# Weight parts, normed input and MLP activations: buffers of one kind at one byte modulo 512

## The chip, the cores and the metric

One core of one Trainium2 chip runs the whole program. The metric is the device time of one execution in microseconds; the median of three runs of the kernel before is 2125.77 us (2125.0 to 2126.07).

## The reference

Two residual layers over 256 tokens of 2048 channels, all in float32. Cut to what matters:

```python
def reference(x, positions, ...):
    for i in range(2):
        if i == 0:      # sparse attention: 16 heads, 4 kv heads, an indexer picks 64 keys a query
            x = x + _dsa_mixer(_rmsnorm(x, attn_norm_g[0]), attn_w_in[0], ..., attn_w_out[0], positions)
        else:           # (B * conv3(C * u)) @ w_out, with B, C, u = h @ w_in
            x = x + _short_conv_mixer(_rmsnorm(x, conv_norm_g[0]), conv_w_in[0], conv_w[0], conv_w_out[0])
        h = _rmsnorm(x, mlp_norm_g[i])
        a = jax.nn.relu(h @ mlp_w1[i])          # 2048 -> 8192
        x = x + (a * a) @ mlp_w2[i]             # 8192 -> 2048
    return x
```

Nearly all of the arithmetic is the products of 256 tokens with the weights.

## The kernel before

**Products.** Weights arrive in float32 by SyncE's DMAs into four `raw` tiles, two pieces in each. `split` turns a piece into two float32r parts: ScalarE writes the high part `wh` (L202), VectorE the rest `wl` (L203). The activations are held as high and low parts too: 16 `xp` tiles for the normed input (one for each 128 rows of the contraction, high parts of 256 tokens, then low parts), four `hq` tiles for four such k-tiles each (attention output, MLP hidden values, convolution output). A product is high times high, plus low times high, plus high times low. `matmuls(p)` issues piece p in one of two forms:

- tall: the weight is the stationary operand (128 columns of it), xp is streamed: L224 with `wh` on 512 columns, L225 with `wl` on 256. A piece is 4 column groups by 2 k-tiles, 8 pairs, 16 matmuls. Used for the first MLP weight and the convolution's input.
- wide: the activations are stationary, the weight is streamed: L229 (high x, `wh`), L230 (low x, `wh`), L231 (high x, `wl`), mostly 512 columns each, four triples, 12 matmuls a piece. Used on hq for the second MLP weight and both output projections, on xp for the attention input.

Each matmul comes with a weight load (LDWEIGHTS, its row in the profile is PEld), which runs beside the matmul before it.

**Order.** Everything is written out by hand, in one sequence of units: attention input (pieces 0 to 63: 16 for the indexer with column groups of 384, 384 and 336, 16 for k and v, 32 for q), attention output (64 to 95), MLP 0 (96 to 351, groups of two tall units of 8 pieces and two wide ones of 8), convolution input (352 to 447, tall), convolution output (448 to 479, wide), MLP 1 (480 to 735). After each piece, `step_all` advances the side work (norms, attention, activations) and pieces up to four ahead are split. So `wh` and `wl` have five buffers each (`AHEAD + 1`), and piece p uses buffer 0, 4, 3, 2, 1, 0, ... for p = 0, 1, 2, 3, 4, 5, ...

**Addresses.** The pool lays its tiles out one after the other in the order of their first use, rounded to 32 bytes, behind the scratch for the descriptors of GpSimd's DMAs (16384 bytes at the default). `wh` and `wl` buffers are `WMAX` = 1104 floats wide, 4416 bytes, which is 8 times 512 and 320 more, so that five buffers of one kind begin at five different bytes modulo 512. In the layout of the kernel before (first byte in a partition, modulo 512):

| tile | buffers | first byte modulo 512 |
| --- | --- | --- |
| ident, x0, x1 | 1 | 128 |
| raw | 4 | 320, 448, 64, 192 |
| xp | 16 | 320, all of them |
| wh | 5 | 320, 128, 448, 256, 64 (buffers 0 to 4) |
| wl | 5 | 384, 192, 0, 320, 128 (buffers 0 to 4) |
| tmp | 18 | 448, all of them |
| hq | 4 | 0, all of them |
| half | 4 | 0, all of them |

Inside a buffer, the slices that a matmul reads begin at multiples of 512 bytes (128 floats) in the tall form and in xp and hq.

Of the kernel before, what the change touches and what calls it, by code (L numbers as in the profile page):

```python
# [27 lines left out]
RAWS = 4  # L28
NTMP = 18
WMAX = 1104  # L30
START = 12
IDX_PAUSE = 2
K_PAUSE = 3
# [4 lines left out]
QIW = [384, 384, 336]  # L38


# 500000 ** -(j / 16), j = 0..15, then 500000 ** -(j / 8), j = 0..7, in float32
_F16 = [
    1.0, 0.44036659598350525, 0.1939227432012558, 0.08539710193872452, 0.03760603070259094,
    0.016560440883040428, 0.007292664609849453, 0.0032114461064338684, 0.0014142135623842478,
# [7 lines left out]


class Unit:
    """One accumulation group over K, in ticks of kk k-tiles, on n columns of a weight.

    wide: out[token, column], banks of the given column widths for each of two token tiles.
    tall: out[column, (token by x high part, token by x low part)], a bank for 128 columns.
    """

    def __init__(self, src, kk, widths, ticks, lhs, end, tall=False):
        self.src, self.kk, self.widths, self.ticks = src, kk, widths, ticks
# [6 lines left out]
def trunk(ctx: ExitStack, tc: tile.TileContext, x, positions, attn_norm_g, attn_w_in, attn_q_norm_g,  # L69
# [13 lines left out]
    def sbt(shape, tag, bufs, dt=F32):  # L83
        return sb.tile(shape, dt, name=nm(tag), tag=tag, bufs=bufs)

    def tmp():
        return sbt([P, 512], "tmp", NTMP)

    def small(n, dt=F32):
        return sbt([P, 32], "small", 20, dt)[:, :n]  # L90

# [1 line left out]
    live = []  # L93
    done = set()
    tp_used = [0]
# [34 lines left out]
        while not all(k in done for k in keys):  # L130
            yield

# [1 line left out]
    ident = sb.tile([P, P], F32, name="ident")  # L134
    xs = [sb.tile([P, D], F32, name=f"x{t}") for t in range(2)]
    xr = x[0].rearrange("(t p) d -> t p d", p=P)
# [18 lines left out]
    nc.gpsimd.dma_start(gq, attn_q_norm_g[0:1, :].to_broadcast([P, HD]))  # L155
    nc.gpsimd.dma_start(gk, attn_k_norm_g[0:1, :].to_broadcast([P, HD]))

# [1 line left out]
    units = []  # L159
    raws = []  # L160
    raw_tiles = {}
# [29 lines left out]
    def split(p):  # L191
        if p >= len(pieces):
            return
        u, i, r = pieces[p]
        w = u.kk * u.n
        src = raw_tiles[r][:, (i % 2) * w : (i % 2 + 1) * w]
        hi = sbt([P, WMAX], "wh", AHEAD + 1, F32R)
        lo = sbt([P, WMAX], "wl", AHEAD + 1, F32R)
        c = 0
        for v in u.widths if p == 0 else [w]:  # L200
            a = slice(c, c + v)
            nc.scalar.activation(hi[:, a], src[:, a], AF.Copy)  # L202
            nc.vector.tensor_tensor(lo[:, a], src[:, a], hi[:, a].bitcast(F32), ALU.subtract)  # L203
            c += v
        piece_tiles[p] = (hi, lo)
        if p + 1 == len(pieces) or pieces[p + 1][2] != r:
            del raw_tiles[r]
            load(r + RAWS)
# [22 lines left out]
                        nc.tensor.matmul(o[:, :w], ah, wl, start=False, stop=(k == K - 1))  # L231
                c += w

# [1 line left out]
    def rsqrt(v, n):  # L235
        """v**-0.5 for a [P, n] tile, by a bit guess and three Newton steps."""
        y, t = small(n), small(n)
        yi = y.bitcast(I32)
        nc.vector.tensor_scalar(yi, v.bitcast(I32), 1, None, op0=ALU.logical_shift_right)
        nc.vector.tensor_scalar(yi, yi, -1, 0x5F3759DF, op0=ALU.mult, op1=ALU.add)  # L240
        for _ in range(3):
            nc.gpsimd.tensor_tensor(t, y, y, ALU.mult)  # L242
            nc.gpsimd.tensor_tensor(t, t, v, ALU.mult)
            nc.gpsimd.tensor_scalar(t, t, -0.5, 1.5, op0=ALU.mult, op1=ALU.add)
            nc.gpsimd.tensor_tensor(y, y, t, ALU.mult)
        return y

# [1 line left out]
    def norm_gen(st, half):  # L249
        """Operand tiles of x*g for k-tiles of one half, and its part of the squares' sum."""  # L250
        if st["key"] != "attn":
            yield
        elif half == 1:
            yield from wait(("attn", 0, "T"))
        def take(k0, ps):
            for j in range(2):
                k = k0 + j
                g = st["g"][:, k : k + 1]
                xp = sbt([P, 512], "xp", KT, F32R)
                hi, lo = xp[:, 0:256], xp[:, 256:512]  # L260
                src = ps[:, j * 256 : (j + 1) * 256]
                nc.scalar.activation(hi, src, AF.Copy, scale=g)
                nc.vector.scalar_tensor_tensor(  # L263
                    lo, src, g, hi.bitcast(F32), op0=ALU.mult, op1=ALU.subtract
                )
                st["T"][k] = xp
            tp_put()

        prev = None
        for k0 in range(half * 8, half * 8 + 8, 2):  # L270
            if prev is not None and (tp_used[0] >= TP or st["key"] == "attn" and k0 == 2):
                take(*prev)
                prev = None
                yield
            ps = yield from tp_get()
            for j in range(2):
                for t in range(2):
                    nc.tensor.transpose(  # L278
                        ps[:, j * 256 + t * P : j * 256 + (t + 1) * P],
                        xs[t][:, (k0 + j) * P : (k0 + j + 1) * P],  # L280
                        ident,
                    )
            if prev is not None:
                take(*prev)
            prev = (k0, ps)
            yield
        take(*prev)
        done.add((st["key"], half, "T"))
        yield from pause(4)
        for q in range(2):  # L290
            for t in range(2):
                junk = tmp()
                c = (half * 2 + q) * 512
                nc.scalar.activation(
                    junk, xs[t][:, c : c + 512], AF.Square,
                    accum_out=st["ss"][:, t * 4 + half * 2 + q : t * 4 + half * 2 + q + 1],
                )
            yield
        done.add((st["key"], half))
# [11 lines left out]
        done.add((st["key"], "rs"))  # L311

    def norm_rows(key, power):
        """The token scale (or its square) of a norm along the free axis, [P, 256]."""
        st = norms[key]
        yield from wait((key, "rs"))
        yield from pause(3)
# [47 lines left out]
        force(lambda: (key, "rs") in done)  # L365
        return norms[key]["rs"][:, t : t + 1]

# [1 line left out]
    def add_to_x(nh, then=None, store=False, norm=None):  # L369
        def end(banks):  # L370
            for t in range(2):
                for b in range(2):
                    # the last bank of all leaves in two parts
                    w = 256 if store and nh and t and b else 512
                    for o in range(0, 512, w):
                        c = nh * 1024 + b * 512 + o
                        sl, ps = xs[t][:, c : c + w], banks[t][b][:, o : o + w]
                        if norm is None:
                            nc.vector.tensor_tensor(sl, ps, sl, ALU.add)
                        else:  # L380
                            rs_of(norm, t)
                            nc.vector.scalar_tensor_tensor(  # L382
                                sl, ps, norms[norm]["rs2"][:, t : t + 1], sl, op0=ALU.mult, op1=ALU.add
                            )
                        if store:
                            nc.sync.dma_start(out[0][t * P : (t + 1) * P, c : c + w], sl)
# [8 lines left out]

        return src

# [1 line left out]
    rope = sb.tile([P, 2, 4, RH + RI], F32, name="rope")  # L399
    NF = RH + RI  # L400

    def rope_tables():
        """rope[:, t, 0:4] = cos, cos, -sin, sin of position * frequency."""
        yield from pause(10)
        pf = small(2)
        nc.vector.tensor_copy(pf, posi)
# [20 lines left out]
        nc.vector.tensor_scalar(rope[:, :, 2], rope[:, :, 3], -1.0, None, op0=ALU.mult)  # L427

    def rotate(v, t, heads, half, off):
        """Partial rotary on v [P, heads, dim] in place: its first 2*half dims."""  # L430
        c = rope[:, t, 0:2, off : off + half].unsqueeze(1).to_broadcast([P, heads, 2, half])
        ns = rope[:, t, 2, off : off + half].unsqueeze(1).to_broadcast([P, heads, half])
        s = rope[:, t, 3, off : off + half].unsqueeze(1).to_broadcast([P, heads, half])
# [119 lines left out]
        done.add("bias")  # L553

    def head_scale(sq, n, mul):
        """(mean of squares + eps)**-0.5 * mul from a list of squared [P, n*HD] tiles."""
        v = small(n * len(sq))
        for i, s in enumerate(sq):
            nc.vector.tensor_reduce(
# [77 lines left out]
    def q_gen(n, qs, sqs):  # L637
# [14 lines left out]
            qT[t] = q  # L652
        qs = None
        yield from wait("bias", "kT")
        # scores; a chunk is (token tile, heads, keys)
        chunks = [(0, (0, 1, 2, 3)), (1, (0, 1)), (1, (2, 3))]
        sims = yield from tp_get(3)
        for (t, hs), ps in zip(chunks, sims):
# [73 lines left out]
        done.add(("o", n, 0))  # L732
        done.add(("o", n, 1))

# [1 line left out]
    Q = {}  # L736

    def hq():
        return sbt([P, 2048], "hq", 4, F32R)

    def quad_lhs(key, k0=0):
# [5 lines left out]
        return lhs  # L747

    def put_pair(key, q, i, val):
        """Split [P, (2, 256)] fp32 into k-tiles 2i, 2i+1 of a quad."""  # L750
        if i == 0:
            Q[key, q] = hq()
        v = Q[key, q].rearrange("p (j c) -> p j c", c=512)[:, 2 * i : 2 * i + 2]
# [4 lines left out]
        done.add((key, q, i))  # L758

    def fold(dst, ps):  # L760
        """dst [P, 256] = the sum of a tall bank's two halves."""
        h = sbt([P, 256], "half", 4)
        nc.scalar.activation(h, ps[:, 256:512], AF.Copy)  # L763
        nc.vector.tensor_tensor(dst, ps[:, 0:256], h, ALU.add)  # L764
# [4 lines left out]
            fold(r[c // 2][:, c % 2 * 256 : (c % 2 + 1) * 256], banks[0][c])  # L769
        return r  # L770

# [1 line left out]
    def m1_end(key, q):  # L773
        def end(banks):
            live.append(h_gen(key, q, fold4(banks)))
# [6 lines left out]
            put_pair(key, q, i, r[i])  # L782
            yield

# [1 line left out]
    C = {}  # L786

    def c_end(q):
# [55 lines left out]
            put_pair("by", q, i, y[i])  # L844
            yield

# [1 line left out]
    W2 = [512, 512]  # L848
    W4 = [128] * 4
    wi = attn_w_in[0]  # L850
# [33 lines left out]
        ))  # L884
    add_mlp(1, None, True)

# [1 line left out]

    def load_x(a, b):
        for t in range(2):  # L890
# [12 lines left out]
    for r in range(2, RAWS):  # L903
        load(r)

    # transposes of no use but to have the tensor engine's clock up when x arrives
    ps = bank()
    for _ in range(START):
        nc.tensor.transpose(ps[:, 128:256], ident, ident)
# [55 lines left out]
```

## Time and profile before

| | us |
| --- | --- |
| median of three runs | 2125.77 (2125.0 to 2126.07) |
| span of the profiled execution | 2122.9 |
| TensorE busy (matmuls) | 2112.0, 99% |
| weight loads | 1788.8, 84% |
| VectorE busy | 1286.4, 61% |
| ScalarE busy | 977.2, 46% |
| GpSimd busy | 114.8, 5% |
| DMA | 392.66 MB, mean 185 GB/s |

The profile gives the execution's time from its first to its last instruction, the span; the runs' times have what lies around it as well. A matmul's end is modelled and lies behind the start of the next one, so its row's duration (392 ns for 512 columns) is not what it costs TensorE: that is the distance from its start to the start of the next. The rows that carry this are in the section on rows below.

### The profile page before, as it was taken

What the parts mean: (1) busy time and instruction counts of PE and PEld (TensorE: products, weight loads), DVE (VectorE), ACT (ScalarE), POOL (GpSimd) and SP (SyncE); (2) the same over time, 40 slices, a digit from 0 to 9 for tenths busy, and PEclk for the clock granted to TensorE, in tenths of its full rate; (3) what the DMA queues carried; (4) which work ended last, traced back from release to release, by engine and by line L of the source; (5) the groups of instructions that cost most, each with busy time, mean ns of one, the idle gap of its engine ahead of it and who ended that gap; (6) DMA issues with size and microseconds to landing.
All of it is one profiled execution on the core that took longest, in us unless ns stands there. A gap on an engine that the chain in (4) does not pass through costs nothing.

```text
span 2122.9 us, 26675 instructions
## 1 busy us (share of the span) xinstructions
PE 2112.0 (99%) x10714; PEld 1788.8 (84%) x10714; DVE 1286.4 (61%) x1553; ACT 977.2 (46%) x1271; POOL 114.8 (5%) x220
## 2 busy tenths in 40 slices
PE   9999999999999999999999999999999999999999
PEld 8878778888888888888888888888888888888887
DVE  5587656655656556556666566556565565655654
ACT  5456545443444434444555454454444344443443
POOL 0333100000000000000011110001000000000000
PEclk9999999999999999999999999999999999999999
DMA  8544455556555565565555555556655566555653
GB/s 274 173 141 163 139 177 170 188 184 206 183 189 189 180 205 181 189 198 179 183 194 179 198 179 190 196 169 202 195 184 191 181 198 193 183 190 188 199 186 111
DMA packets 152268, 392.66 MB, mean 185 GB/s; under 512 B 6368, under 2 KB 7088, under 8 KB 152144
## 3 DMA queue, kind: packets, MB, share of 16 engines
q1 hardware_dynamic: 151888, 390.75, 56.6%
q8 instruction: 84, 1.38, 0.2%
q0 software_dynamic: 224, 0.19, 0.1%
q14 instruction: 40, 0.33, 0.0%
q10 hardware_dynamic: 32, 0.01, 0.0%
HBM read 388.83 MB, written 2.10 MB: 184 GB/s over the span
## 4 chain that ended last, share of the span: by engine, by line
PE 98%; POOL 1%; DMA 1%; DVE 0%; ACT 0%; issue 0%; SPq 0%; DVEq 0%; ACTq 0%
PE ps L224 30%; PE ps L230 16%; PE ps L231 16%; PE ps L229 16%; PE ps L225 16%; DMA raw<-in_attn_w_in 1%; PE ps L278 1%; PE ps L661 0%; PE ps L507 0%; PE ps L719 0%; PE ps L706 0%; POOL tmp L440 0%; POOL rot L436 0%; PE ps L646 0%; POOL tmp L439 0%; ACT wh L202 0%
## 5 line engine op out<-in xcount | busy, mean ns | idle before, releaser
L203 DVE TENSOR_TENSOR wl<-raw,wh 128x1024 fp32r<-128x1024 f32 (+2 forms) x738 | 890.1, 1225 | 551.7 <-ACT wh L202 551.1
L202 ACT ACTIVATE wh<-raw 128x1024 fp32r<-128x1024 f32 (+2 forms) x738 | 765.9, 1055 | 722.8 <-PE ps L230 390.2
L224 PE MATMUL ps<-xp,wh 128*128 128x512 f32 x2816 | 978.0, 392 | 0.0
L225 PE MATMUL ps<-xp,wl 128*128 128x256 f32 x2816 | 786.9, 279 | 0.0
L224 PEld LDWEIGHTS ps<-xp,wh 128*128 128x128 f32 x2816 | 529.8, 188 | 114.6
L225 PEld LDWEIGHTS ps<-xp,wl 128*128 128x128 f32 x2816 | 531.6, 189 | 0.8
L231 PE MATMUL ps<-wl,hq 128*128 128x512 f32 x1280 | 505.0, 395 | 0.0
L229 PE MATMUL ps<-wh,hq 128*128 128x512 f32 x1280 | 505.0, 395 | 0.0
L230 PE MATMUL ps<-wh,hq 128*128 128x512 f32 x1280 | 505.0, 395 | 0.0
L229 PEld LDWEIGHTS ps<-wh,hq 128*128 128x128 f32 x1280 | 240.9, 188 | 55.7 <-issue 0.5
L230 PEld LDWEIGHTS ps<-wh,hq 128*128 128x128 f32 x1280 | 240.3, 188 | 56.3 <-issue 0.5
L231 PEld LDWEIGHTS ps<-wl,hq 128*128 128x128 f32 x1280 | 240.7, 188 | 54.8
L764 DVE TENSOR_TENSOR tmp<-ps,half 128x256 f32<-128x256 f32 x176 | 74.7, 424 | 110.0 <-ACT half L763 110.0
L763 ACT ACTIVATE half<-ps 128x256 f32<-128x256 f32 x176 | 67.6, 384 | 152.3 <-PE ps L225 152.3
L382 DVE SCALAR_TENSOR_TENSOR x<-ps,rs_mlp,x 128x512 f32<-128x512 f32 x129 | 90.8, 746 | 53.0 <-PE ps L231 53.0
L229 PE MATMUL ps<-wh,xp 128*128 128x512 f32 (+2 forms) x288 | 114.2, 397 | 2.2 <-ACT wh L202 2.0
L230 PE MATMUL ps<-wh,xp 128*128 128x512 f32 (+2 forms) x288 | 108.0, 375 | 0.9 <-DVE xp L263 0.9
L231 PE MATMUL ps<-wl,xp 128*128 128x512 f32 (+2 forms) x288 | 108.1, 375 | 0.4 <-DVE wl L203 0.4
L756 ACT ACTIVATE hq<-tmp 128x512 fp32r<-128x512 f32 x72 | 45.5, 632 | 105.4 <-DVE tmp L781 93.0
L757 DVE TENSOR_TENSOR hq<-tmp,hq 128x512 fp32r<-128x512 f32 x72 | 51.1, 710 | 50.3 <-ACT hq L756 50.3
L242 POOL TENSOR_TENSOR small<-small 128x8 f32<-128x8 f32 (+1 forms) x27 | 14.0, 517 | 1011.3 <-DVE small L240 1009.7
L229 PEld LDWEIGHTS ps<-wh,xp 128*128 128x128 f32 x288 | 54.6, 190 | 12.5 <-ACT wh L202 2.4
(131 smaller groups left out, 661.9 us busy)
## 6 DMA issues: line engine op xcount, KB each, us to landing
raw<-in_mlp_w SPq DMA_DIRECT2D x256, 1024.0 KB, 5.4
raw<-in_conv_w_in SPq DMA_DIRECT2D x48, 1024.0 KB, 5.2
raw<-in_attn_w_in SPq DMA_DIRECT2D x24, 1024.0 KB, 5.3
raw<-in_attn_w_out SPq DMA_DIRECT2D x16, 1024.0 KB, 5.4
raw<-in_conv_w_out SPq DMA_DIRECT2D x16, 1024.0 KB, 5.4
raw<-in_attn_w_in SPq DMA_DIRECT2D x5, 1104.0 KB, 8.2
raw<-in_attn_w_in SPq DMA_DIRECT2D x5, 552.0 KB, 8.7
out_y<-x SPq DMA_DIRECT2D x7, 256.0 KB, 2.9
```

The lines of the kernel that those rows point to most:

```text
L202: nc.scalar.activation(hi[:, a], src[:, a], AF.Copy)
L203: nc.vector.tensor_tensor(lo[:, a], src[:, a], hi[:, a].bitcast(F32), ALU.subtract)
L224: nc.tensor.matmul(o, wh, xk, start=(k == 0), stop=False)
L225: nc.tensor.matmul(o[:, 0:256], wl, xk[:, 0:256], start=False, stop=(k == K - 1))
L229: nc.tensor.matmul(o[:, :w], ah, wh, start=(k == 0), stop=False)
L230: nc.tensor.matmul(o[:, :w], al, wh, start=False, stop=False)
L231: nc.tensor.matmul(o[:, :w], ah, wl, start=False, stop=(k == K - 1))
L382: nc.vector.scalar_tensor_tensor(sl, ps, norms[norm]["rs2"][:, t : t + 1], sl, op0=ALU.mult, op1=ALU.add)
L756: nc.scalar.activation(hi, val, AF.Copy)
L757: nc.vector.tensor_tensor(lo, val, hi.bitcast(F32), ALU.subtract)
L763: nc.scalar.activation(h, ps[:, 256:512], AF.Copy)
L764: nc.vector.tensor_tensor(dst, ps[:, 0:256], h, ALU.add)
```

## The change

The tiles `wh` and `wl` become 1152 floats wide (4608 bytes, 9 times 512) in place of 1104. Three unused tiles are put between others in the pool: 448 bytes ahead of `wh`, 64 bytes ahead of `wl`, 256 bytes ahead of `hq`. To make room, the scratch for GpSimd's DMA descriptors goes from 16384 bytes to 4096. Comments and docstrings go; no instruction is added, removed or moved.

```diff
 WMAX = 1104
+WPITCH = 1152
...
+    def shift(n):
+
+        sb.tile([P, n // 4], F32, name=nm("shift"))
...
-        hi = sbt([P, WMAX], "wh", AHEAD + 1, F32R)
-        lo = sbt([P, WMAX], "wl", AHEAD + 1, F32R)
+        if p == 0:
+            shift(448)
+        hi = sbt([P, WPITCH], "wh", AHEAD + 1, F32R)
+        if p == 0:
+            shift(64)
+        lo = sbt([P, WPITCH], "wl", AHEAD + 1, F32R)
...
     def hq():
+        if not Q:
+            shift(256)
         return sbt([P, 2048], "hq", 4, F32R)
...
-    nc = bacc.Bacc("TRN2", target_bir_lowering=False, num_devices=1)
+    nc = bacc.Bacc("TRN2", target_bir_lowering=False, num_devices=1, dynamic_dma_scratch_size=4096)
```

## Rows read from the trace of the kernel before

**Rows 1.** The page: busy time, granted clock in 40 slices (tenths).
```profile
PE 2112.0 (99%) x10714; PEld 1788.8 (84%) x10714; DVE 1286.4 (61%) x1553; ACT 977.2 (46%) x1271; POOL 114.8 (5%) x220
...
PEclk9999999999999999999999999999999999999999
```

**Rows 2.** TensorE's waits, the longest of six (us in total, times, longest).
```profile
PE ps L229 <- ACT wh L202: 2.0, 1, 2.0
```

**Rows 3.** Groups by line and shape, TensorE: xcount | busy us, mean ns | idle before.
```profile
L224 PE MATMUL ps<-xp,wh 128*128 128x512 f32 x2816 | 978.0, 392 | 0.0
...
L229 PE MATMUL ps<-wh,hq 128*128 128x512 f32 x1280 | 505.0, 395 | 0.0
...
L229 PE MATMUL ps<-wh,xp 128*128 128x512 f32 x192 | 81.1, 422 | 0.0
```

**Rows 4.** Timeline (start us, us): first L224 of tall pieces 405 to 410, 430.
```profile
1195.02 0.39 PE L224 MATMUL ps<-xp,wh 128*128 128x512 f32 x1
...
1197.80 0.39 PE L224 MATMUL ps<-xp,wh 128*128 128x512 f32 x1
...
1200.57 0.39 PE L224 MATMUL ps<-xp,wh 128*128 128x512 f32 x1
...
1203.31 0.39 PE L224 MATMUL ps<-xp,wh 128*128 128x512 f32 x1
...
1206.08 0.40 PE L224 MATMUL ps<-xp,wh 128*128 128x512 f32 x1
...
1208.88 0.39 PE L224 MATMUL ps<-xp,wh 128*128 128x512 f32 x1
...
1264.29 0.39 PE L224 MATMUL ps<-xp,wh 128*128 128x512 f32 x1
```

**Rows 5.** Timeline of all engines, inside piece 407.
```profile
1201.60 0.39 PE L224 MATMUL ps<-xp,wh 128*128 128x512 f32 x1
1201.61 0.19 PEld L225 LDWEIGHTS ps<-xp,wl 128*128 128x128 f32 x1
1201.83 0.28 PE L225 MATMUL ps<-xp,wl 128*128 128x256 f32 x1
...
1201.88 0.42 DVE L764 TENSOR_TENSOR tmp<-ps,half 128x256 f32<-128x256 f32 x1 [1.68 <-ACT half L763]
...
1202.96 0.39 PE L224 MATMUL ps<-xp,wh 128*128 128x512 f32 x1
```

**Rows 6.** Timeline: first L229 of wide pieces 152 to 157, last triple of 154.
```profile
488.35 0.40 PE L229 MATMUL ps<-wh,hq 128*128 128x512 f32 x1
...
491.13 0.39 PE L229 MATMUL ps<-wh,hq 128*128 128x512 f32 x1
...
493.94 0.39 PE L229 MATMUL ps<-wh,hq 128*128 128x512 f32 x1
...
496.01 0.39 PE L229 MATMUL ps<-wh,hq 128*128 128x512 f32 x1
...
496.71 0.39 PE L229 MATMUL ps<-wh,hq 128*128 128x512 f32 x1
...
499.47 0.40 PE L229 MATMUL ps<-wh,hq 128*128 128x512 f32 x1
...
502.26 0.40 PE L229 MATMUL ps<-wh,hq 128*128 128x512 f32 x1
```

**Rows 7.** Timeline: first L229 of wide pieces 38, 39 and 40, on xp.
```profile
138.59 0.39 PE L229 MATMUL ps<-wh,xp 128*128 128x512 f32 x1
...
141.36 0.39 PE L229 MATMUL ps<-wh,xp 128*128 128x512 f32 x1
...
144.13 0.40 PE L229 MATMUL ps<-wh,xp 128*128 128x512 f32 x1
```

**Rows 8.** The page: DMA queue of GpSimd (packets, MB, share of 16 engines).
```profile
q0 software_dynamic: 224, 0.19, 0.1%
```

**Rows 9.** Busy us (count) by engine, granted clock, DMA share, GB/s in a stretch.
```profile
1150.00:1300.00 150.00, 150.00 (x869) 132.36 (x868) 95.25 (x118) 72.88 (x98) 11.33 (x8) 1.00 0.57 188
```

## The prediction, before the result was known

> **What bounds the kernel now.** I read the page's summary first: TensorE is busy 99% of the span [rows 1]. Then the table of TensorE's waits: it has six entries, each met once, the longest 2.0 us [rows 2]. So the time is the number of matmuls times the distance from the start of one to the start of the next, and no other engine sets it. [...] The groups by line give the numbers [rows 3]: 2816 pairs of the "tall" form (L224 with 512 columns, each followed by L225 with 256), 1280 triples of the "wide" form on hq (L229, L230, L231; one of the three lines is shown), and in the attention input 288 triples on xp, 192 of them with 512 columns. In pieces: 352 tall ones of 8 pairs, 320 wide ones of 4 triples on hq, and 64 wide ones on xp, 48 of which have 4 triples of 512 columns.
>
> Busy time hides what counts here, because the ends of matmuls are modelled and overlap; I went by starts in the timeline. Five tall pieces in a row, identical in instructions, shapes and engine clock, start at 1195.02, 1197.80, 1200.57, 1203.31, 1206.08, and the next at 1208.88 [rows 4]: they last 2.78, 2.77, 2.74, 2.77 and 2.80 us. The pattern returns with period five: 25 pieces take 1264.29 - 1195.02 = 69.27 us, 2.771 us each [rows 4]. A unit has 8 pieces, a group of raw tiles 8, the xp tiles repeat by 8 or 16; only wh and wl have five buffers. The first of these pieces is number 405, so it has buffer 0, and the others 4, 3, 2, 1 (the order in which the pool hands them out). What differs between them is where the buffer begins. Call r the first byte of wh minus that of the activation operand, modulo 512 (wl is 64 further in every buffer). Against xp at 320 the five pieces have r = 0, 256, 448, 128 and 320, so 448 is the fastest and 320 the slowest.
>
> Inside the fastest piece, 2.74 us from 1200.57 on [rows 4], the first pairs are slower; from 1201.60 to 1202.96 four pairs take 1.36 us, 0.340 each, with the weight load of the next matmul starting beside each matmul [rows 5]. A VectorE instruction in the middle [rows 5] changes nothing in the pace.
>
> Wide pieces on hq show the same thing: the pieces from 488.35 on last 2.78, 2.81, 2.77, 2.76 and 2.79 us [rows 6], mean 2.782. Here hq begins at 0, so r = 256, 448, 128, 320 and 64. On xp, with other absolute bytes but again r = 128 and then 320, two undisturbed pieces last 2.77 and 2.77 us (138.59 to 141.36 to 144.13) [rows 7], against 2.77 and 2.76 on hq. So the distance between the two operands carries the length, not the absolute byte.
>
> **What the change does, part by part.**
> Addresses first, all modulo 512. The smaller scratch moves everything down by 12288 bytes, 24 times 512: nothing changes. xp stays at 320 and ends at 320; 448 bytes put wh at 256, and the pitch of 1152 floats (4608 bytes, 9 times 512) keeps all five buffers there; 64 more put wl at 320, all five again. tmp moves from 448 to 320, the small tiles behind it by the same 128 bytes, and 256 more put hq, and half behind it, at 128. So r against xp is 448 in every piece, and r against hq is 128.
>
> Tall pieces: 256, 320 and 320 for wh, wl and xp are the very bytes that buffer 3 has now, in the fastest of the five pieces. Without another relation before it, no piece has slow first pairs: 8 x 0.340 = 2.720 us instead of 2.771, 0.051 x 352 = 17.9 us. After a change from wide to tall (17 times) the first pairs stay slow, as in the 2.74 us that such a piece takes now: 17 x 0.02 = 0.3 us. Sum: 17.6 us less. The worse bound is that each piece keeps 2.74: 0.031 x 352 = 10.9 us less.
>
> Wide pieces on hq: r = 128 is buffer 1 now, 2.77 us. Its first triples follow another relation; its last one (496.01 to 496.71) takes 0.70 us [rows 6], the three before it 0.69 each. The steady piece is therefore between 4 x 0.69 = 2.76 and 4 x 0.70 = 2.80; I take 2.772, near its own row: 0.010 x 320 = 3.2 us less, bounds 7.0 us less and 5.8 us more.
>
> Wide pieces on xp: r = 448 there, which on hq lasts 2.81 us, the slowest: 0.028 x 48 = 1.3 us more, and up to 2 us with the 16 narrower pieces. Transposes and small matmuls break up many of these pieces, so the lower bound is nothing. I take 1.2 us more.
>
> Edits with one answer. No instruction is added or taken away. The seven DMAs of GpSimd, which use the scratch, move 224 packets in all [rows 8] over 16 engines; they are issued at the start and TensorE waits for none of them: nothing, and if the smaller ring held them up, at most a few us of a stretch in which TensorE has other work. tmp, small tiles, half: their users are ScalarE and VectorE, off the path. If TensorE is 1 to 2% quicker, VectorE goes from 95.25 busy us of 150 to 65% in a tall stage, the DMA share from 0.57 to 0.58 [rows 9]: cover enough, nothing is late next. The kernel stays bound by the same matmuls.
>
> [...]
>
> Sum: -17.6 - 3.2 + 1.2 = -19.6 us. The profiled span is 2122.9 us, the median of the runs 2125.8, so 2.9 us lie around the span and do not change: span 2103.3, time 2106.2 us.
>
> **Rivals.**
> 1. The wide pieces lock in. The relation on hq is never shaken, and the steady state turns out like the slowest, 2.81 us. For it: pieces visibly carry something over from the piece before. Against: buffer 1's own triples stay at 0.69 to 0.70. Then 0.028 x 320 = 9.0 us more in place of 3.2 less: -17.6 + 9.0 + 1.2 = -7.4, 2118.4 us.
> 2. It does not do what it says: the lengths go with the buffer number for another reason (which buffer ScalarE and VectorE fill meanwhile, which also turns with five), or with address bits above 512. [...] For it: rows 4 alone cannot part buffer number from address. Against: the pace in rows 5 is the same with VectorE running and not, and r = 128 gives the same length on hq and xp. Time 2125.8 us.
> 3. Slower. Today five relations take turns, and each piece starts afresh; with one relation for good, the two read streams settle into whatever collision that relation allows, in tall pieces too. Place: every tall and wide piece. Price: 2.80 - 2.771 = 0.029 x 352 = 10.2 us, 9.0 us on hq and 1.2 on xp, 20.4 us more: 2146.2 us. It decides once a steady tall pair costs over 2.771 / 8 = 0.346 us. For it: the first pairs of each piece depend on the piece before. Against: the last pairs of the fastest piece stay at 0.340 without drift.
>
> **How the numbers follow.** Forecast 80%, rival 1 7%, rival 2 8%, rival 3 5%. The range reaches from both gains at their best (-17.9 - 7.0 = -24.9, 2100.9) to the tall gain at its worse bound with nothing on hq (-10.9 + 1.2, 2116), drawn in to 2115 because both ends together are unlikely: 2101 to 2115 us. That leaves out the rivals, 20%. Faster by over 0.2% (4.3 us, about what a measurement of this kernel can tell from no change) holds for the forecast and rival 1: 87%. Within 0.2%: rival 2, 8%. Slower: rival 3, 5%.
>
> **What would show it.** Right: in the tall stages all pieces start 2.72 us apart, with no period of five; on hq about 2.77 us; on xp the undisturbed pieces near 2.81; instruction counts and TensorE's short table of waits unchanged. Wrong: a period of five that stays (rival 2); pieces all alike but at 2.77 or more in tall stages (rival 3); hq pieces at 2.80 or more (rival 1); a new entry of many us among TensorE's waits, for wh, wl or raw, which would mean that other work has become the bound.

## The result, and the profile after

The changed kernel takes 2106.52 us (median of four runs, 2105.35 to 2108.39), 0.9912 of the kernel before, 95% interval 0.9898 to 0.9926: 19 us less. A second series of runs gave 2106.07 us (2105.4 to 2106.35) and 0.9908 (0.9891 to 0.9924). The forecast was 2106.2 us, with a range of 2101 to 2115.

The page of the profiled execution (span 2106.5 us), its lines for busy time and the granted clock, answering [rows 1]:

```profile
PE 2094.5 (99%) x10714; PEld 1776.9 (84%) x10714; DVE 1286.8 (61%) x1553; ACT 977.2 (46%) x1271; POOL 114.4 (5%) x220
...
PEclk9999999999999999999999999999999999999999
```

The counts are those of before, and so are the busy times of VectorE, ScalarE and GpSimd; only TensorE's moved. The two longest of TensorE's five waits, answering [rows 2]:

```profile
PE ps L238 <- ACT wh L211: 2.0, 1, 2.0
PE ps L238 <- ACT xp L271: 1.6, 1, 1.6
```

So TensorE still waits for nearly nothing, and what changed is the distance between starts. The timeline of the same tall pieces as in [rows 4], 405 to 410 and 430 (start us, us):

```profile
1188.32 0.39 PE L233 MATMUL ps<-xp,wh 128*128 128x512 f32 x1
...
1191.04 0.39 PE L233 MATMUL ps<-xp,wh 128*128 128x512 f32 x1
...
1193.76 0.39 PE L233 MATMUL ps<-xp,wh 128*128 128x512 f32 x1
...
1196.48 0.39 PE L233 MATMUL ps<-xp,wh 128*128 128x512 f32 x1
...
1199.20 0.39 PE L233 MATMUL ps<-xp,wh 128*128 128x512 f32 x1
...
1201.92 0.39 PE L233 MATMUL ps<-xp,wh 128*128 128x512 f32 x1
...
1256.32 0.39 PE L233 MATMUL ps<-xp,wh 128*128 128x512 f32 x1
```

2.72 us five times; the period of five is gone, and 25 pieces take 68.00 us in place of 69.27. The wide pieces on hq, 152 to 157, answering [rows 6]:

```profile
489.91 0.39 PE L238 MATMUL ps<-wh,hq 128*128 128x512 f32 x1
...
492.69 0.39 PE L238 MATMUL ps<-wh,hq 128*128 128x512 f32 x1
...
495.46 0.39 PE L238 MATMUL ps<-wh,hq 128*128 128x512 f32 x1
...
498.23 0.39 PE L238 MATMUL ps<-wh,hq 128*128 128x512 f32 x1
...
501.00 0.39 PE L238 MATMUL ps<-wh,hq 128*128 128x512 f32 x1
...
503.78 0.39 PE L238 MATMUL ps<-wh,hq 128*128 128x512 f32 x1
```

2.77 to 2.78 us, where they had been 2.78, 2.81, 2.77, 2.76, 2.79. And on xp, pieces 38 to 40, answering [rows 7]:

```profile
141.40 0.39 PE L238 MATMUL ps<-wh,xp 128*128 128x512 f32 x1
...
144.21 0.39 PE L238 MATMUL ps<-wh,xp 128*128 128x512 f32 x1
...
147.03 0.39 PE L238 MATMUL ps<-wh,xp 128*128 128x512 f32 x1
```

2.81 and 2.82 us: these got longer, from 2.77.

Added up over all pieces, from the starts in nanoseconds, the two profiled executions differ like this; "undisturbed" are pieces with no wait and with no other matmul between theirs or just before them.

| pieces | before, all, us | after, all, us | difference | undisturbed before, us each | undisturbed after, us each |
| --- | --- | --- | --- | --- | --- |
| 352 tall | 981.7 | 964.4 | -17.3 | 2.771 (335 pieces) | 2.721 (335) |
| 320 wide on hq | 905.4 | 902.8 | -2.6 | 2.782 (295) | 2.773 (295) |
| 48 wide on xp, 512 columns | 167.2 | 167.4 | +0.2 | 2.777 (14) | 2.813 (14) |
| 16 wide on xp, narrower (the first) | 55.7 | 59.0 | +3.3 | 3.018 (6) | 3.027 (6) |

The sum is -16.4 us, the difference of the spans. The last row is the kernel's start, where the first pieces wait for x and the weights; two things made it longer in this execution. The second piece took 6.34 us for 4.56: TensorE waited in it 1.6 us for xp (the line above) and 0.7 us for wl, where it had been 0.2 and 0.4:

```profile
PE ps L229 <- ACT xp L262: 0.2, 1, 0.2
```

The third took 6.23 us for 4.69. It runs from 19.0 to 25.2 us, with the same wait of 0.9 us in it as before, and for a part of that time TensorE's granted clock was down: 0.66 from 20 to 25 us where it had been 1.00, with 19 matmuls where there had been 33, after 5 us in which TensorE was busy for 2.83 (whether the one led to the other is not shown). The two stretches after (busy us and count by engine, then the granted clock, DMA share and GB/s), and the second of them before:

```profile
15.00:20.00 5.00, 2.83 (x17) 2.33 (x16) 1.37 (x2) 1.49 (x2) 0.00 (x0) 1.00 1.03 420
20.00:25.00 5.00, 4.61 (x19) 4.60 (x20) 3.01 (x5) 3.22 (x5) 0.00 (x0) 0.66 0.99 390
```

```profile
20.00:25.00 5.00, 5.00 (x33) 4.99 (x32) 3.73 (x5) 2.38 (x5) 0.00 (x0) 1.00 1.02 417
```

No run shows that the change brings either. In the second series' profile the clock was 1.00 from 20 to 25 us and the same 16 pieces take 56.8 us, at a span of 2104.5 us, with the other rows at 964.4, 902.8 and 167.7; with the smaller scratch alone (the first experiment) they take 55.2 us.

VectorE was forecast to stay far from being the limit. It is busy for 98.55 us of 150 in a tall stage, answering [rows 9], 66% where 65% was forecast:

```profile
1150.00:1300.00 150.00, 150.00 (x884) 132.77 (x883) 98.55 (x121) 74.27 (x100) 11.41 (x8) 1.00 0.59 194
```

### The profile page after: what moved, and what is told of

Read it like the earlier page. It is cut to its first block, busy times and chain, and to the rows that moved or that the text cites. A ratio compares the mean times of both kernels' runs of the same rounds, so it can differ in the third digit from the quotient of the medians.

```text
span 2106.5 us, 26675 instructions
## 1 busy us (share of the span) xinstructions
PE 2094.5 (99%) x10714; PEld 1776.9 (84%) x10714; DVE 1286.8 (61%) x1553; ACT 977.2 (46%) x1271; POOL 114.4 (5%) x220
## 4 chain that ended last, share of the span: by engine, by line
PE 99%; DMA 1%; DVE 0%; SPq 0%; ACT 0%; issue 0%; DVEq 0%
PE ps L233 30%; PE ps L240 17%; PE ps L238 17%; PE ps L239 17%; PE ps L234 15%; PE ps L287 1%; DMA raw<-in_attn_w_in 1%; PE ps L670 0%; PE ps L516 0%; PE ps L728 0%; PE ps L715 0%; PE ps L655 0%; SPq L902 0%; DVE x L391 0%; PE ps L497 0%; DVE wl L212 0%
## 5 line engine op out<-in xcount | busy, mean ns | idle before, releaser
L233 PE MATMUL ps<-xp,wh 128*128 128x512 f32 x2816 | 960.7, 390 | 0.0
L234 PE MATMUL ps<-xp,wl 128*128 128x256 f32 x2816 | 777.5, 276 | 0.0
```

Of the source, the lines that this page charges most:

```text
L233: nc.tensor.matmul(o, wh, xk, start=(k == 0), stop=False)
L234: nc.tensor.matmul(o[:, 0:256], wl, xk[:, 0:256], start=False, stop=(k == K - 1))
```

## Experiments

Theory: the distance between the two operands that TensorE reads, modulo some power of two, sets the steady length of a piece. Rivals: the absolute byte; the buffer number or what other engines write meanwhile; a fixed relation as such; the smaller scratch. In all tables below, r is the first byte of wh minus that of the activation operand, d that of wl minus wh; lengths are distances between the first starts of neighbouring pieces.

**The scratch alone.** The kernel before with

```diff
-    nc = bacc.Bacc("TRN2", target_bir_lowering=False, num_devices=1)
+    nc = bacc.Bacc("TRN2", target_bir_lowering=False, num_devices=1, dynamic_dma_scratch_size=4096)
```

> The kernel before with the smaller scratch alone: all addresses move by 24 times 512 bytes. Theory: nothing changes, 2125 to 2126 us, with the period of five in the tall pieces (2.78, 2.77, 2.74, 2.77, 2.80). Rival (the scratch or the absolute place brings part of the gain): up to 19 us less.

2124.23 us, beside 2125.9 for the kernel before on the same chip. All pieces as before: 981.7 us tall, 905.4 us on hq, to the tenth, with lengths of 2.774, 2.775, 2.736, 2.770 and 2.800 by buffer. The 1.7 us are within the spread of the kernel before, whose runs in another series took 2124.06 to 2127.69 us. The scratch brings nothing.

**Another absolute byte.** The changed kernel with

```diff
+                if k == 0:
+                    shift(192)
                 xp = sbt([P, 512], "xp", KT, F32R)
```

> The changed kernel with 192 more bytes ahead of xp, which moves xp, wh, wl, tmp, hq and half by 192 bytes together: every distance between operands of the large matmuls stays, every absolute byte modulo 512 is another. Theory (distance): tall pieces 2.721, wide on hq 2.773, on xp 2.813, time within the spread of the changed kernel, 2105 to 2109. Rival (absolute bytes, as of a line or a row of the memory): other lengths, between 2.70 and 2.80.

2105.39 us; tall 2.721, on hq 2.773, on xp 2.813. Tall pieces 405 and 410, 13.60 us apart:

```profile
1185.40 0.39 PE L233 MATMUL ps<-xp,wh 128*128 128x512 f32 x1
...
1199.00 0.39 PE L233 MATMUL ps<-xp,wh 128*128 128x512 f32 x1
```

With every large operand at another byte modulo 512, the lengths are those of the changed kernel (2.721, 2.773 and 2.813): this move of 192 bytes kept the distances, and the lengths stayed with them. It also answers what the trace of before could only suggest, with r = 128 on hq and on xp. Since 192 is three times 64, the place of an operand within 64 bytes stayed as it was; no run moves that without changing a distance.

**256 bytes between hq and wh.** The changed kernel with

```diff
     def hq():
-        if not Q:
-            shift(256)
```

> The changed kernel without the 256 bytes ahead of hq: hq begins at 384 in place of 128, so r on hq is 384 in place of 128, and half moves with it. Theory with period 256: wide pieces on hq stay at 2.773 and the time stays within 2105 to 2109. Theory with period 512: another length, unknown, between 2.76 and 2.81, a change of -4 to +12 us. Tall pieces 2.721 in both.

2107.40 us; on hq 2.773 us, 902.8 us in all, as in the changed kernel. Pieces 152 and 157, 13.87 us apart:

```profile
489.07 0.39 PE L238 MATMUL ps<-wh,hq 128*128 128x512 f32 x1
...
502.94 0.39 PE L238 MATMUL ps<-wh,hq 128*128 128x512 f32 x1
```

On hq, r = 384 and r = 128 take the same 2.773 us, as a period of 256 has it, and this third of the change had no effect of its own.

**Many distances in one run.** The changed kernel with buffers of 1280 floats, each unit reading its parts at its own offset:

```diff
-WPITCH = 1152
+WPITCH = 1280
...
+        u.oh, u.ol = 0, 0
+        if u.tall or u.first >= 64:
+            form = TALL if u.tall else WIDE
+            r, d = form[sum(v.first >= 64 and v.tall == u.tall for v in units[:-1]) % len(form)]
+            at = (320 if u.tall else 128) + r
+            u.oh, u.ol = (at - 256) % 512 // 4, (at + d - 320) % 512 // 4
...
-        hi = sbt([P, WPITCH], "wh", AHEAD + 1, F32R)
+        hi = sbt([P, WPITCH], "wh", AHEAD + 1, F32R)[:, u.oh : u.oh + w]
...
-        lo = sbt([P, WPITCH], "wl", AHEAD + 1, F32R)
+        lo = sbt([P, WPITCH], "wl", AHEAD + 1, F32R)[:, u.ol : u.ol + w]
```

TALL and WIDE (not printed here) list the pairs (r, d), one for each unit.

> The changed kernel with wider wh and wl buffers (1280 floats), in which every unit reads its weight parts at an offset of its own: the 44 tall units go through r (wh minus activation operand, modulo 512) of 0, 64, ... 448 with wl 64, 0, 128, 192 and 256 bytes behind wh, the 36 wide units on hq through the same list as far as it goes. Nothing else is changed. Theory (the distance between the two operands sets the pace): with wl 64 behind, steady tall pieces of 2.72 us at r = 448, 2.77 to 2.78 at 0, 128 and 256, 2.80 at 320; steady wide pieces 2.773 at 128 and about 2.81 at 448, 2.78 to 2.79 at 0, 64, 256 and 320. If the period is 256, r = 64, 192 and 384 in tall units repeat 320, 448 and 128 (2.80, 2.72, 2.77). No forecast for the other distances of wl. Rival (buffer number, or what is written meanwhile): all tall units stay at 2.72 and all wide ones at 2.77, since buffers and writers are as in the changed kernel.

The run took 2132.15 us. Two units at r = 192 and r = 320 with d = 64: pieces 138 and 143, then 170 and 175 of the timeline, five pieces apart.

```profile
450.80 0.39 PE L241 MATMUL ps<-xp,wh 128*128 128x512 f32 x1
...
464.40 0.39 PE L241 MATMUL ps<-xp,wh 128*128 128x512 f32 x1
...
539.52 0.39 PE L241 MATMUL ps<-xp,wh 128*128 128x512 f32 x1
...
553.65 0.39 PE L241 MATMUL ps<-xp,wh 128*128 128x512 f32 x1
```

13.60 us and 14.13 us: 2.72 and 2.83 each. Median lengths of the undisturbed pieces from the third of each unit on, in ns (where other matmuls stand between the pieces of a unit, a cell rests on as few as three):

| tall, d | r = 0 | 64 | 128 | 192 | 256 | 320 | 384 | 448 |
| --- | --- | --- | --- | --- | --- | --- | --- | --- |
| 0 | 2830 | 2827 | 2806 | 2792 | 2830 | 2827 | 2806 | 2792 |
| 64 | 2773 | 2800 | 2774 | 2720 | 2773 | 2827 | 2773 | 2720 |
| 128 | 2800 | 2827 | 2819 | 2826 | 2800 | 2827 | 2819 | 2826 |
| 192 | 2810 | 2800 | 2826 | 2773 | 2773 | 2720 | 2773 | 2773 |

| wide on hq, d | r = 0 | 64 | 128 | 192 | 256 | 320 | 384 | 448 |
| --- | --- | --- | --- | --- | --- | --- | --- | --- |
| 0 | 2720 | 2747 | 2790 | 2800 | 2720 | 2747 | 2790 | 2800 |
| 64 | 2783 | 2773 | 2773 | 2813 | 2782 | 2786 | 2773 | 2814 |
| 128 | 2747 | 2765 | 2747 | 2771 | 2773 | 2761 | 2747 | 2771 |
| 192 | 2747 | 2773 | 2787 | 2773 | 2747 | 2773 | 2787 | 2773 |

The lists went on to d = 256: wide at r = 0 to 192: 2720, 2747, 2790, 2800, as at d = 0; tall at r = 0 to 448: 2830, 2827, 2807, 2825, 2773, 2827, 2807, 2825, which is not what d = 0 gave at 192, 256 and 448. Tall with d = 384, r = 0 to 192: 2800, 2827, 2814, 2773, where d = 128 gave 2826 for the last.

The distance matters, as expected; the buffer number and the writers, the same in every unit, do not explain lengths between 2720 and 2830. Columns 256 apart agree within 1 ns in 25 of 32 pairs: in these a period of 256 in r shows again. With d = 64 the tall row came out as forecast but at 320 (2827, not 2800), the wide row but at 64 (2773). The cells in which two columns 256 apart differ (tall: d = 64 at 64 and 320, d = 192 at 0 and 256, at 64 and 320 and at 128 and 384; wide: d = 64 at 64 and 320, d = 128 at 0 and 256 and, by 4 ns, at 64 and 320) are the first sign that a distance has more than one steady length. That d too counts modulo 256 is not shown for the tall form. For the wide form a better relation than that of the change shows up: r = 0, d = 0, with 2720.

**A fixed relation by itself.** The changed kernel without its three shifts; only the pitch of 1152 is left:

```diff
-        if p == 0:
-            shift(448)
...
-        if p == 0:
-            shift(64)
...
-        if not Q:
-            shift(256)
```

> The changed kernel without its three shifts: all buffers of a kind still begin at one byte (wh, wl and xp at 320, hq at 384), so the relation is as fixed as in the changed kernel, but it is another. Theory (which relation counts, by the scan): tall pieces 2.830 us each, 38 us more than the changed kernel, wide pieces on hq 2.800, 9 us more, undisturbed ones on xp 2.72: 2145 to 2155 us, slower than the kernel before. Rival (a fixed relation helps by itself, because no piece has to settle anew): 2106 to 2126 us.

2129.94 us in one run, where the kernel before took 2124.57: slower, but by 5 us and not by the 20 or more that I expected. On hq the pieces were as the scan had them (2.800), on xp too (2.722), but the tall ones took 2.774 us, not 2.830. Pieces 405, 410 and 430, then 152 and 157 on hq:

```profile
1196.94 0.39 PE L229 MATMUL ps<-xp,wh 128*128 128x512 f32 x1
...
1210.81 0.39 PE L229 MATMUL ps<-xp,wh 128*128 128x512 f32 x1
...
1266.28 0.39 PE L229 MATMUL ps<-xp,wh 128*128 128x512 f32 x1
...
488.05 0.39 PE L234 MATMUL ps<-wh,hq 128*128 128x512 f32 x1
...
502.05 0.39 PE L234 MATMUL ps<-wh,hq 128*128 128x512 f32 x1
```

13.87 and 55.47 us for 5 and 20 tall pieces, 14.00 for 5 wide ones. The rival falls: with one relation throughout, the kernel is slower than with five taking turns (tall +0.8 us, hq +5.8 us in all against before). And 2.774 against 2.830 at the same r = 0, d = 0 is the second sign of more than one length.

**Finer steps.** The scan again with lists in steps of 16 bytes:

```diff
-TALL = [(0, 64), (64, 64), (128, 64), ...]
+TALL = [(256, 64), (272, 64), (288, 64), ..., (448, 0), (448, 16), ...]
-WIDE = [(0, 64), (64, 64), ...]
+WIDE = [(0, 0), (16, 0), ..., (0, 16), (0, 32), ...]
```

> The scan again in steps of 16 bytes: tall units with wl 64 behind and r from 256 to 496, then r = 448 with wl 0 to 240 behind, then twelve units that repeat relations of the first scan after other neighbours; wide units with wl at wh and r from 0 to 240, then r = 0 with wl 16 to 240 behind, then five repeats. Theory: the short lengths (2.72) sit in bands some tens of bytes wide round r = 448 with wl 64 behind (tall) and r = 0 with wl at wh (wide); nothing is below 2.72, since 2.720 is met in both forms. Relations with two lengths in the first scan (r = 320 with wl 64 behind: 2.80 in the kernel before, 2.83 in the scan; 320 with wl 192: 2.72 against 2.80 at 64) go by what came before them. Rival: single lines of 64 bytes are what counts, so steps of 16 or 32 bytes within one change nothing.

2130.14 us. Nothing below 2720 was found, in either form. The good spots met are narrow: tall, d = 64, r = 432, 448, 464: 2800, 2720, 2826; wide, d = 0, r = 240, 0, 16: 2720, 2720, 2780. So the tall one is no band of some tens of bytes, and in neither does one length hold for the 64 bytes from 448 or from 0; but each neighbour was tried in one unit only, and might have a shorter length too. And r = 448 with d = 64, the relation of the change, took 2720 in three units of this run but 2800 in all eight pieces of the one that came after r = 448, d = 48. Likewise r = 320, d = 192: 2827 in one unit, 2720 in another; r = 0, d = 0: 2773 and 2830. Some cells in which the first scan's columns 256 apart differed came out alike here: tall r = 320, d = 64 took 2827 once more and then twice 2800, the length at 64, and wide r = 320, d = 64 took 2773 twice, the length at 64.

**Does a longer length stay?** The scan's code with the changed kernel's pitch and relations, but three odd units (the lists written shorter here):

```diff
-WPITCH = 1280
+WPITCH = 1152
+TALL = [(448, 64)] * 44
+TALL[16] = TALL[28] = (448, 48)
+TALL[22] = (320, 64)
+WIDE = [(128, 64)]
```

> The changed kernel with three of its 44 tall units at another relation: the first of the convolution's twelve (wl 48 behind wh in place of 64), the seventh of them (r = 320), and the first of the second MLP (wl 48 behind). All others, and all wide units, are as in the changed kernel. Theory (a relation allows several steady lengths, and the one before decides which): the convolution's units two to six stay at 2.80 us a piece, 40 pieces, with the very addresses that give 2.72 in the changed kernel; units eight to twelve are back at 2.72; in the second MLP the unit after the odd one is at 2.80, and after the next wide units all are at 2.72 again. That is 48 x 0.08 = 3.8 us more, and 1 to 2 us for the odd units: 2109 to 2114 us. Rival (the relation alone sets the length, the 2.80 of the fine scan was something else): every unit but the three at 2.72 after its first piece, 2106 to 2109 us.

2110.94 us, and piece for piece as the theory had it. The timeline of the convolution's units (start us, us): piece 360, at 1062.74, is the first with the changed kernel's own bytes; 368, 369 and 399 follow on them; 400, at 1175.63, is the first of the second odd unit; 408, at 1198.04, is back on the changed kernel's bytes, and so are 409 and 416.

```profile
1062.74 0.40 PE L241 MATMUL ps<-xp,wh 128*128 128x512 f32 x1
...
1086.03 0.40 PE L241 MATMUL ps<-xp,wh 128*128 128x512 f32 x1
...
1088.83 0.40 PE L241 MATMUL ps<-xp,wh 128*128 128x512 f32 x1
...
1172.83 0.40 PE L241 MATMUL ps<-xp,wh 128*128 128x512 f32 x1
...
1175.63 0.39 PE L241 MATMUL ps<-xp,wh 128*128 128x512 f32 x1
...
1198.04 0.40 PE L241 MATMUL ps<-xp,wh 128*128 128x512 f32 x1
...
1200.77 0.39 PE L241 MATMUL ps<-xp,wh 128*128 128x512 f32 x1
...
1219.81 0.39 PE L241 MATMUL ps<-xp,wh 128*128 128x512 f32 x1
```

1086.03 to 1175.63 are 32 pieces, 2.800 us each; 1200.77 to 1219.81 are 7 pieces, 2.720 each. Same bytes, same instructions, two steady lengths, and only the unit before differs. The 40 pieces kept the longer one to the end of their stretch, across one in which other matmuls stood between theirs. In the second MLP the unit after the odd one was at 2.800 too; two wide units later, all were at 2.720.

**TensorE alone.** The changed kernel with

```diff
         u, i, r = pieces[p]
+        if p >= 480:
+            piece_tiles[p] = kept[p % 5]
+            return
...
-        piece_tiles[p] = (hi, lo)
+        piece_tiles[p] = kept[p % 5] = (hi, lo)
```

> The changed kernel in which the second MLP's weights (pieces 480 to 735) are not split: its matmuls read the last five pairs of buffers again, and no weight DMA, ScalarE split or VectorE split runs beside them. This leaves out part of the computation. Theory (TensorE's two own read streams collide): pieces stay at 2.721 and 2.773. [...]

2105.82 us, no change. In the stretch from 1480 to 1600 us VectorE and ScalarE have fallen to 21 and 8 busy us, and the DMA share to nothing (busy us by engine, columns as in [rows 9]):

```profile
1480.00:1600.00 120.00, 120.00 (x634) 102.85 (x633) 21.34 (x36) 8.42 (x18) 0.00 (x0) 1.00 0.00 1
```

In its timeline the tall pieces 514 and 519 are 13.59 us apart, 2.72 each:

```profile
1488.33 0.39 PE L237 MATMUL ps<-xp,wh 128*128 128x512 f32 x1
...
1501.92 0.39 PE L237 MATMUL ps<-xp,wh 128*128 128x512 f32 x1
```

Pieces from 496 on have a median of 2.720 tall and 2.773 on hq. So neither DMA nor the splits' reads and writes are in these lengths, nor in the 0.053 us by which the two differ.

**One relation for each form.** What the scan pointed to: the changed kernel with

```diff
     def hq():
         if not Q:
-            shift(256)
+            shift(448)
...
         hi = sbt([P, WPITCH], "wh", AHEAD + 1, F32R)
+        if not u.tall:
+            hi = hi[:, 16 : 16 + w]
```

> The changed kernel with one relation for each form: tall pieces keep theirs (wh 64 before xp, wl at xp), wide pieces read wh 64 bytes further on, so that wh, wl and the activation operand (xp at 320; hq, by 448 in place of 256 bytes ahead of it, at 320 too) all begin at the same byte. Theory (the distance sets the pace, by the scan): tall 2.721 us a piece as before, wide on hq 2.720 in place of 2.773, 17 us less, undisturbed pieces on xp 2.72 in place of 2.813, 1 to 5 us less: 2083 to 2090 us. Rival (the short lengths in the scan came from the change of relation between units and don't last): wide pieces drift back to 2.77 or more, 2105 us or above.

2087.61 us (five runs, 2086.8 to 2088.97), 0.9825 of the kernel before (0.9812 to 0.9839): another 18 to 19 us, about as much again as the change brought, with no instruction changed. Pieces 405 and 410 (tall), 152 and 157 (hq), 38 and 39 (xp):

```profile
1175.58 0.39 PE L235 MATMUL ps<-xp,wh 128*128 128x512 f32 x1
...
1189.18 0.39 PE L235 MATMUL ps<-xp,wh 128*128 128x512 f32 x1
...
482.49 0.39 PE L240 MATMUL ps<-wh,hq 128*128 128x512 f32 x1
...
496.09 0.39 PE L240 MATMUL ps<-wh,hq 128*128 128x512 f32 x1
...
138.57 0.39 PE L240 MATMUL ps<-wh,xp 128*128 128x512 f32 x1
...
141.29 0.39 PE L240 MATMUL ps<-wh,xp 128*128 128x512 f32 x1
```

2.72 us in all three. Over all pieces: 964.1 us tall, 886.8 on hq (16.0 less than the changed kernel), 164.8 on xp. It lasted; the rival falls.

**The changed kernel again**, for its ratio:

> The changed kernel again, for its ratio in more rounds: 2105 to 2109 us, ratio to the kernel before 0.990 to 0.993; tall pieces 2.721, wide on hq 2.773. What changes from run to run lies ahead of the first steady piece, within 20 us of the start.

2106.07 us, 0.9908; pieces as before.

## Why the prediction was right, point by point

- *The bound.* Right: TensorE's starts alone moved, and the other engines' waits took nothing back.
- *Addresses.* Right: the period of five is gone, with 2.72 us five times where 2.74 to 2.80 took turns.
- *Tall pieces.* Right: 2.720 was forecast, 2.721 measured, 17.3 us less where 17.6 were summed. The reason I gave was incomplete, though. I took the last pairs of the fastest piece for the steady state of that relation. They are one of at least two: with the unit at r = 448, d = 48 before it, the same relation stays at 2.800 for 40 pieces. Had the changed kernel's tall pieces all stayed at that longer length, 352 x 0.029 = 10 us would have been lost where 17 were gained (an estimate; no run has it). It enters its tall units from the attention output and the wide units at r = 128 on hq, and each time fell into the shorter one. The rows of the kernel before do not show that it would; to that extent the term was luck.
- *Wide pieces on hq.* Right: 2.773 for 2.772. The term came to 2.6 us, not 3.2, since 0.008 rather than 0.010 us a piece was gained.
- *Wide pieces on xp.* The length was right (2.813 us undisturbed, for 2.81), the sum not: 1.2 us were summed and 0.2 and 0.5 measured in the two series, since only 14 of the 48 pieces run undisturbed.
- *The sum.* The three terms measured give -17.3 - 2.6 + 0.2 = -19.7 us where -19.6 were summed. That is closer than the terms themselves, whose misses of 0.3, 0.6 and 1.0 us cancel by luck. The start, which the sum put at nothing, changes by more than these from run to run: its 16 pieces take 55.0 to 59.0 us in the profiled executions of all runs.
- *Scratch, small tiles, headroom.* Nothing, as forecast; the scratch alone was run.
- *Other engines.* Right: they do not set the lengths, and the run with TensorE alone agrees: 2.720 and 2.773 us with and without their traffic. What moves the lengths is where the operands begin, from 2.720 to 2.830 us a piece in the first scan.
- *Rival 1* (hq pieces lock in at 2.81): didn't happen, 2.773. *Rival 2* (not the address): falls by the runs with the scratch alone (for bits above 512), with many distances and with TensorE alone. My argument for the distance, r = 128 on both operands, held.
- *Rival 3* (settling for good into a longer length) fell for this change, but a longer length that stays was measured (2.800 us for 40 pieces, with the three odd units), and I dismissed it with an argument that could not tell: pairs that stay at one pace without drift are what the longer length of the same relation shows as well. In the run with the pitch alone it happened on hq (2.800 a piece, for 2.782 before) and the whole was slower than the kernel before. Five percent was little for it.
- *The modulus.* I called it 512, as the change does; in r, the runs show 256 where they show a period (2.773 us on hq at r = 128 and 384, and 25 of 32 pairs of the first scan).

What stays open: why the distance counts. That two operand reads of TensorE collide is a theory of mine; no run shows it. What the runs show is that distances between the operands count (2.720 to 2.830 us a piece in the first scan), while a move of all by 192 bytes (2.721, 2.773 and 2.813 us as before) and the other engines' work (2.720 and 2.773 us without it) don't. Nor is the lengthening confined to the matmul beside which wl is loaded: moving wl alone (r = 448, d = 64 to 128, in the first scan) lengthened the spacing after both matmuls of a pair, from 227 to 236 ns after the 512 columns with the load of wl beside them and from 113 to 117 ns after the 256 columns with the load of wh. What makes a unit fall into one of its lengths or the other is open too: the runs show only that it goes by what ran before.

## What to carry to other kernels

Where a profile shows TensorE busy throughout and waiting for nobody (here 99% of the span, the longest wait 2.0 us), read the starts of its matmuls, not their durations: a length that repeats with the number of buffers points at the buffers' bytes (here 2.74 to 2.80 us a piece, with a period of five). Then vary the distance between the operands unit by unit inside one kernel, for each form of matmul by itself; one such run gives a first map, in which a distance that has two lengths shows one of them (here r = 448 with d = 64: 2.720 us in the first scan, 2.800 us for 40 pieces with the three odd units). Choose for each form the distance with the shortest length measured, check that it is reached from whatever runs before it, and don't take a fixed relation for a good one: the pitch alone took 2129.94 us where the kernel before took 2124.57.

## What the runs showed of the hardware that was not expected

- With the float32r operands of this kernel, the distance between the moving and the stationary operand moved the steady pace by 4% in the first scan, from 2.720 to 2.83 us for the 6144 columns of a piece, at a mean granted clock of 0.999; 256 bytes more or less between wh and the activation operand made no difference in 25 of 32 pairs. In the scan with finer steps 16 bytes made the difference (2720 to 2780 ns on hq from r = 0 to 16, 2720 to 2826 in tall pieces from r = 448 to 464).
- Many of the lengths measured are 26 or 27 ns a piece apart: 2720, 2747, 2773, 2800, 2827 in the first scan. No piece that ran undisturbed was steadily below 2720 in these runs, in the tall form with 16 matmuls or the wide one with 12: 226.7 ns for 512 columns, 113.3 for 256.
- One distance had two steady lengths (2720 and 2800 ns at r = 448, d = 64, with the three odd units); the longer held for 40 pieces, 112 us, and only the unit before differed.
- How the first 25 us go moves the span by up to 4 us, a fifth of what the change is worth: the 16 narrower pieces take 55.0 to 59.0 us in the profiled executions of all runs. In the one of 59.0 us the granted clock was 0.66 from 20 to 25 us; in that of the kernel before, 55.7 us, and that of the second series, 56.8 us, it was 1.00 there.
